# One SBUF input per VectorE instruction in a top-k search, and three query tiles moved between the tiles of a convolution

## The chip, the core and the metric

The kernel runs on one core of one Trainium2 chip, all in float32. The metric is the device time of one execution in microseconds, a median of several runs. The profile is of one execution; its times are counted from the span's first instruction. Engines are named as in the profile: PE is TensorE, PEld its weight loads, DVE is VectorE, ACT is ScalarE, POOL is GpSimd, SP is the engine that issues the transfers.

## The reference

One step of a two-layer encoder for a prompt of 1024 positions and a sample of 64 positions (with 512 cached ones), model width 1024. Layer 0 is what the change touches:

```
h = rmsnorm(x) * (1 + scale(c)) + shift(c)
q, k, v, ga, qi, ki, wi, gb, gc, xin, gz = split(h @ w_in)
score[q, s] = sum_h wi[q, h] * relu(qi[q, h] . ki[s])          # admissible keys only
keep the top 256 keys of each query (144 for the sample)
a = softmax(q . k / 8 over the kept keys) v * silu(ga)          # 8 heads of 64, 2 groups of keys
b = gb * conv3(gc * xin) * silu(gz)                             # causal, 3 taps
x += gate(c) * (concat(a, b) @ w_out)
```

Layer 1 is a gated unit with a spatial mix in chunks of 128 positions, and a final norm follows. Keys, values, index keys and the convolution's state are outputs too.

## The kernel before

The activations lie with features on partitions: 8 k tiles of 128 features by 1088 columns (1024 of the prompt, 64 of the sample). To be exact in float32, each operand is split into a high and a low part (`ah`, `al`, `w_hi`, `w_lo`), and a product is three matrix products. A column tile of a projection is 128 output features: 3 chunks of columns (364, 364, 360) by 8 k tiles by 3 products, so 72 matrix products. For each tile the weights come by a transfer from SP, ACT makes `w_hi` (L239), POOL makes `w_lo` (L240, two inputs), PE multiplies (L248, or L263 where the products are handed out a step at a time), and ACT moves each chunk from PSUM to SBUF (L784, L793).

Layer 0 goes through these stages. `scores` fills `S`, 128 partitions by 4800 columns: seven row blocks of 128 queries with 384, 512, 640, 768, 896, 1024 and 576 keys. `topk` then finds the k-th largest score of each row bit by bit: 8 rounds for the exponent, 23 for the mantissa, 31 in all. In a round the scores smaller than a candidate are counted row block by row block, then a few instructions on 1 to 4 columns decide the bit: `m` (L571), the step `g` (L578 for the exponent, L588 for the mantissa) and the candidate (L579, L590). There are three groups of row blocks (`GROUPS`) that go on independently. The four blocks of 512, 640, 768 and 576 keys are counted by VectorE in all rounds. Those of 896 and 1024 keys are counted by ACT in all rounds (a sum of signs, L565 and L568). That of 384 keys is counted by VectorE in the first 15 rounds and by ACT in the last 16. In the first 15 rounds the counts read `bias`, a bfloat16 copy of the scores' upper halves with k's sign (L529, one tensor input). In the last 16 they read `S` itself and multiply by k's sign on the way:

```
V.scalar_tensor_tensor(o, self.S[:, span(j)], col(sgn, j), thr.to_broadcast([P, SW[j]]),
                       op0=OP.mult, op1=OP.is_lt, accum_out=col(cv, j))
```

This is L531. Its second tensor input is the threshold, one column broadcast over the block, also in SBUF. All small tensors of the search (`cv`, `m`, `limd`, `lima`, `g`, `cand`, `step`) lie in SBUF.

Beside the search run 14 projection tiles: Q0, K, V, and for each quarter c of the convolution's features GZ (c > 0), GC and XIN. `gc` and `z`, where GC and XIN go, have one buffer each; K and V use them first. `conv` (L758 to L772) runs on POOL alone and ends with `bo *= y`. While it reads `gc` and `z`, the next GC tile can't be moved out of PSUM; there are five PSUM banks for these tiles, so PE can run five chunks ahead. When the thresholds `T` are there, `mask` (L614 to L619) turns each row block of `S` into 0 for chosen keys and a large negative number for the others, in `bias`, on VectorE alone.

Then comes attention, four head pairs with nine row blocks each: logits on PE (L632), bias and maximum on VectorE (L634), exponential on ACT (L637), the normalisation on POOL (L639), transposes and weighted values on PE (L662, L670). The queries of a pair are first stacked by `pair_stack` (ACT L710, POOL L711). Between the products of attention PE does the steps of the tiles in `ATTN_TILES`, one at a time, by fixed numbers (`RATE`). What is left is done behind attention. The first `BEFORE` = 255 steps are done ahead of attention: the tiles Q1, Q2 and Q3 with 72 each, and 39 of GB0.

The instructions are traced in program order, `topk` ahead of the tiles that run beside it. A planner with its own costs then sets the order on each engine, by readiness and then by program order. On the chip each engine keeps to that order.

Of the kernel before, what the change touches and what calls it, by code (L numbers as in the profile page):

```python
# [32 lines left out]
# chunks of columns: of the projections, and of those back to the residual, where a short one comes last  # L33
# [6 lines left out]
def pieces(w):  # L40
    """First columns of the pieces of 128 that cover w columns."""
    return [*range(0, w - P, P), w - P]


# column tiles of the even layer's projection, in the order in which they are computed
# [3 lines left out]
ATTN_TILES = [(Q_, 1), (Q_, 2), (Q_, 3), (GB, 0), (GB, 1), (GA, 0), (GB, 2), (GA, 1), (GB, 3), (GA, 2), (GA, 3)]  # L49


def even_tiles():
    col = {QI: 1280, KIWI: 1792, GA: 768, K_: 512, V_: 640, Q_: 0, GC: 2376, XIN: 2888, GB: 1864, GZ: 3400}
    order = [(QI, 0), (QI, 1), (QI, 2), (QI, 3), (KIWI, 0), (Q_, 0)] + [(GZ, c) for c in range(NGZ)]
    order += [(K_, 0), (V_, 0)]
    for c in range(4):
        order += [(GZ, c)] * (c >= NGZ) + [(GC, c), (XIN, c)]
# [10 lines left out]
# widths of the score rows: prompt blocks 2..7, then the sample  # L68
# [5 lines left out]
# k tiles of late modulation units done after the last two tiles of index queries  # L74
ADA_EARLY = (0, 27)
# gate tiles that fill the waits of the index scores
NGZ = 1
# products that keep the tensor engine's clock up while it waits for 1/rms and for the first modulation
WARM = (7, 3)
# the rows of each search that goes on by itself, and whether ScalarE counts in the first stage and in the second  # L80
# [3 lines left out]
UPPER_ACT = (4, 5)  # L84
SPANS = [slice(min(COL[j] for j in g[0]), max(COL[j] for j in g[0]) + 1) for g in GROUPS]
ORDER = [(0, 1, 2, 3, 4, 5, 6, 7)] + [(7, 0, 6, 1, 5, 2, 4, 3)] * 3
# matrix products of projections that fill the tensor engine's waits: before attention, and for each head pair
# after the logits of a chunk, after a group of weighted values and before it
BEFORE = 255
# [3 lines left out]
def cut(n):  # L93
    """Equal pieces of at most one bank."""
    k = (n + 511) // 512
    return k, n // k


class Trunk:
# [5 lines left out]
    # ------------------------------------------------------------------ helpers  # L105
# [12 lines left out]
    # ------------------------------------------------------------------ constants  # L118
# [21 lines left out]
    # units of 512 modulation columns: u < 4 hold shift and scale of two k tiles each, 4 and 5 the gate  # L140
# [5 lines left out]
    def ada_steps(self, l, u, raw, halt=False):  # L146
        """A unit, a k tile at a step; with halt another step before the transposition."""
# [26 lines left out]
    def ada_late(self, pool):  # L174
        """The units that the index phase leaves room for, a k tile at a step; their loads run ahead."""
# [25 lines left out]
    def pace(self, after, n):  # L201
        """n steps of the side work, behind one of the matrix products."""
# [40 lines left out]
    def product(self, ps, w, c0, c1, kts=range(KT)):  # L243
        """ps [P, c1-c0] = W^T act, in three products of the exact parts."""
# [6 lines left out]
    def steps(self, w, evac, chunks=range(NCH), n=2, tag="pj"):  # L251
        """A projection, n matrix products at a step."""
# [980 lines left out]
```

## Time and profile before

| | us |
|---|---|
| median of 3 runs | 1203.1 (1202.98 to 1203.14) |
| span of the profiled execution | 1200.9 |
| around the span (1203.1 less 1200.9) | 2.2 |
| VectorE busy in the span | 729.0 |
| PE busy in the span | 1098.8 |
| mean granted clock, share of full speed | 0.963 |

The profiled execution has no time of its own beside its span; the median stands for it. A line such as "348.58 2.79 DVE L531 ..." says when an instruction began, how long it took, on which engine and line, what it wrote and read, and in which shape; "x16 | 20.7, 1295 | 0.1" at a row's end is the count, the busy time in us, the mean of one in ns, and the idle time ahead of them.

### The profile page before, as it was taken

Reading aid. Unit: us, or ns where it says so; the run is one execution under the profiler, and the core shown is the slowest. Engines: PE = TensorE matmul, PEld = TensorE weight load, DVE = VectorE, ACT = ScalarE, POOL = GpSimd, SP = SyncE. Lnnn points to the kernel's source line nnn. Section 1 sums busy time; section 2 is a strip of 40 time slices with the busy share of each in tenths; the row PEclk is TensorE's granted clock in tenths of the full one; section 3 lists DMA queues with packets and bytes.
Section 4 is the critical chain, followed back from the end, with each engine's and each line's share of the span. In section 5 each row is a group of like instructions: output and inputs, shape, how many; then the busy total and the mean of one; then the engine's idle time right before and its main releaser. Section 6 shows DMA issues by size and latency. Waiting matters only on the chain.

```text
span 1200.9 us, 18882 instructions
## 1 busy us (share of the span) xinstructions
PE 1098.8 (91%) x7255; PEld 1054.6 (88%) x7255; DVE 729.0 (61%) x1663; ACT 513.6 (43%) x964; POOL 460.2 (38%) x454
## 2 busy tenths in 40 slices
PE   5899999695959885999999899999999999999997
PEld 4799689595958885988999899999999999999996
DVE  5602899999999798776775534431159036346133
ACT  5332784645665525677775533431221211235110
POOL 3632322344647673544542324641133210245121
PEclk9999999898979896999999899999999999999998
DMA  9646401110101010000000350211111210121012
GB/s 362 279 167 220 168 2 53 73 36 19 36 18 36 19 58 14 19 19 19 19 19 19 114 175 1 71 36 36 36 59 40 84 37 19 52 77 65 1 62 88
DMA packets 26074, 81.84 MB, mean 68 GB/s; under 512 B 3072, under 2 KB 9984, under 8 KB 23552
## 3 DMA queue, kind: packets, MB, share of 16 engines
q1 hardware_dynamic: 25984, 80.63, 19.2%
q8 instruction: 57, 0.93, 0.3%
q14 instruction: 33, 0.27, 0.1%
HBM read 74.50 MB, written 6.12 MB: 67 GB/s over the span
## 4 chain that ended last, share of the span: by engine, by line
PE 61%; DVE 25%; ACT 5%; issue 3%; POOL 2%; DMA 2%; SPq 0%; POOLq 0%; DVEq 0%; ACTq 0%
PE pj L248 26%; PE op L248 15%; DVE cum L531 6%; PE pj L263 6%; DVE cum L529 5%; PE av L670 3%; PE logit_ps L632 3%; PE p_ps L662 2%; DVE m L571 2%; PE ada_ps L154 1%; DVE g L588 1%; PE sgu_ps L1048 1%; DVE cum L616 1%; PE first L319 1%; POOL w_lo L240 1%
## 5 line engine op out<-in xcount | busy, mean ns | idle before, releaser
L248 PE MATMUL pj<-ah,w_hi 128*128 128x364 f32 (+1 forms) x984 | 331.0, 336 | 34.4 <-ACT gc L784 33.0
L248 PE MATMUL pj<-al,w_hi 128*128 128x364 f32 (+1 forms) x984 | 328.3, 334 | 0.0
L248 PE MATMUL pj<-ah,w_lo 128*128 128x364 f32 (+1 forms) x984 | 327.5, 333 | 0.0
L240 POOL TENSOR_TENSOR w_lo<-w_raw,w_hi 128x1024 fp32r<-128x1024 f32 x63 | 160.9, 2556 | 380.8 <-ACT w_hi L239 356.8
L248 PEld LDWEIGHTS pj<-ah,w_hi 128*128 128x128 f32 x984 | 188.8, 192 | 36.6 <-ACT gc L784 33.9
L248 PEld LDWEIGHTS pj<-al,w_hi 128*128 128x128 f32 x984 | 188.8, 192 | 0.0
L248 PEld LDWEIGHTS pj<-ah,w_lo 128*128 128x128 f32 x984 | 188.5, 192 | 0.3 <-issue 0.2
L248 PE MATMUL op<-ah,w_lo 128*128 128x448 f32 (+2 forms) x384 | 126.7, 331 | 3.2 <-POOL w_lo L240 3.2
L248 PE MATMUL op<-al,w_hi 128*128 128x448 f32 (+2 forms) x384 | 127.0, 331 | 0.4 <-DVE al L278 0.3
L248 PE MATMUL op<-ah,w_hi 128*128 128x448 f32 (+2 forms) x384 | 127.3, 331 | 0.0
L239 ACT ACTIVATE w_hi<-w_raw 128x1024 fp32r<-128x1024 f32 x69 | 72.7, 1056 | 108.6 <-PE pj L248 79.1
L988 DVE SCALAR_TENSOR_TENSOR x<-op,mod,x 128x192 f32<-128x192 f32 (+2 forms) x64 | 30.5, 497 | 109.0 <-PE op L248 109.0
L263 PE MATMUL pj<-ah,w_hi 128*128 128x364 f32 (+1 forms) x288 | 96.2, 334 | 0.0
L263 PE MATMUL pj<-al,w_hi 128*128 128x364 f32 (+1 forms) x288 | 95.2, 331 | 0.0
L263 PE MATMUL pj<-ah,w_lo 128*128 128x364 f32 (+1 forms) x288 | 95.2, 331 | 0.0
L639 POOL TENSOR_SCALAR S<-S,sm 128x384 f32<-128x384 f32 (+8 forms) x68 | 50.8, 753 | 85.1 <-DVE sm L638 73.7
L248 PEld LDWEIGHTS op<-ah,w_lo 128*128 128x128 f32 x384 | 73.4, 191 | 5.5 <-POOL w_lo L240 3.5
L531 DVE SCALAR_TENSOR_TENSOR cum<-S,sgn,cand 128x512 bf16<-128x512 f32 (+3 forms) x67 | 76.7, 1145 | 1.5
L248 PEld LDWEIGHTS op<-al,w_hi 128*128 128x128 f32 x384 | 73.3, 191 | 3.2 <-DVE al L278 1.1
L248 PEld LDWEIGHTS op<-ah,w_hi 128*128 128x128 f32 x384 | 73.4, 191 | 2.0
L996 POOL TENSOR_TENSOR acc<-acc,sq 128x448 f32<-128x448 f32 (+2 forms) x40 | 40.0, 999 | 91.4 <-ACT sq L994 90.7
L278 DVE TENSOR_TENSOR ptl<-p_ps,pth 128x512 fp32r<-128x512 f32 (+1 forms) x88 | 54.4, 621 | 20.0 <-ACT pth L277 18.7
(251 smaller groups left out, 2120.1 us busy)
## 6 DMA issues: line engine op xcount, KB each, us to landing
w_raw<-in_w SPq DMA_DIRECT2D x53, 512.0 KB, 3.5
ada<-in_ada_w SPq DMA_DIRECT2D x19, 1024.0 KB, 9.1
w_raw<-in_wo SPq DMA_DIRECT2D x16, 512.0 KB, 3.4
x<-in_x SPq DMA_DIRECT2D x8, 544.0 KB, 6.6
bo<-in_ada_w SPq DMA_DIRECT2D x4, 1024.0 KB, 6.8
x<-in_x SPq DMA_DIRECT2D x1, 1792.0 KB, 8.8
out_y<-x SPq DMA_DIRECT2D x1, 1792.0 KB, 6.6
x<-in_x SPq DMA_DIRECT2D x1, 1536.0 KB, 9.2
```

The costliest lines, as they stand in the source:

```text
L239: nc.scalar.activation(hi, raw, AF.Copy)
L240: (nc.gpsimd if lo_eng == "pool" else nc.vector).tensor_sub(lo, raw, hi)
L248: last = self.nc.tensor.matmul(ps, wt[:, kt, :], at[:, kt, c0:c1], start=n == 0, stop=n == len(mms) - 1)
L263: self.nc.tensor.matmul(ps, wt[:, kt, :], at[:, kt, a:b], start=kt == 0 and i == 0, stop=kt == KT - 1 and i == 2)
L278: (lo_eng or self.nc.vector).tensor_sub(lo, src, hi)
L529: V.tensor_scalar(o, self.bias[:, span(j)], thr, 0.0, op0=OP.is_lt, op1=OP.add, accum_out=col(cv, j))
L531: V.scalar_tensor_tensor(o, self.S[:, span(j)], col(sgn, j), thr.to_broadcast([P, SW[j]]), op0=OP.mult, op1=OP.is_lt, accum_out=col(cv, j))
L632: mm = nc.tensor.matmul(pt[:, 0:w], lhs, keys[i][:, g, s], start=i == 0, stop=i == 1)
L639: nc.gpsimd.tensor_scalar(p, p, st[:, 3:4], 0.0, op0=OP.mult, op1=OP.add)
L670: mm = nc.tensor.matmul(av[:, 0:m], self.vs[0:r, vbase + j, g, :], t[0:r, o:o + m], start=j == 0 and i == 0, stop=j == nj - 1 and i == 1)
L988: nc.vector.scalar_tensor_tensor(x[:, t, a:b], ps[:, a:b], self.mod[l][:, 16 + t, j:j + 1], x[:, t, a:b], op0=OP.mult, op1=OP.add)
L996: nc.gpsimd.tensor_add(acc, acc, sq)
```

## The change

Part one, in `topk`. The scores in `S` are multiplied in place by k's sign, once, by ACT; the bfloat16 copy is gone, and all counts of VectorE have the one form that reads `S` and takes the threshold as a scalar pointer. ACT's counts read `S` with a fixed scale. `limd`, `lima`, `g` and `step` move into a bank of PSUM (the one that weighted values use later), so that L571, L588, L590 and their like have one input in SBUF and one in PSUM; `g` is written to PSUM too. `mask` gets one more instruction per row block, on ACT, that gives the scores their own sign back.

Part two. Q1 stands behind V, Q2 behind the first XIN and Q3 behind the second; `BEFORE` is 0, so GB0's 39 steps go to attention's fill. Comments that the diff also removes are left out here.

```diff
-ATTN_TILES = [(Q_, 1), (Q_, 2), (Q_, 3), (GB, 0), (GB, 1), (GA, 0), (GB, 2), (GA, 1), (GB, 3), (GA, 2), (GA, 3)]
+ATTN_TILES = [(GB, 0), (GB, 1), (GA, 0), (GB, 2), (GA, 1), (GB, 3), (GA, 2), (GA, 3)]
-    order += [(K_, 0), (V_, 0)]
+    order += [(K_, 0), (V_, 0), (Q_, 1)]
-        order += [(GZ, c)] * (c >= NGZ) + [(GC, c), (XIN, c)]
+        order += [(GZ, c)] * (c >= NGZ) + [(GC, c), (XIN, c)] + [(Q_, c + 2)] * (c < 2)
-BEFORE = 255
+BEFORE = 0
...
+        small = self.bank("av", "small")
+        limd, lima, g = (small[:, i * NSB:(i + 1) * NSB] for i in range(3))
+        step = small[:, 32:32 + steps * NSB].rearrange("p (s j) -> p s j", j=NSB)
...
-        def smaller(j, thr, first):
-            o = junks[0][:, 0:SW[j]]
-            if first:
-                V.tensor_scalar(o, self.bias[:, span(j)], thr, 0.0, op0=OP.is_lt, op1=OP.add, accum_out=col(cv, j))
-            else:
-                V.scalar_tensor_tensor(o, self.S[:, span(j)], col(sgn, j), thr.to_broadcast([P, SW[j]]),
-                                       op0=OP.mult, op1=OP.is_lt, accum_out=col(cv, j))
+        def smaller(j, thr):
+            V.tensor_scalar(junks[0][:, 0:SW[j]], self.S[:, span(j)], thr, 0.0, op0=OP.is_lt, op1=OP.add,
+                            accum_out=col(cv, j))
...
-        top = self.S.bitcast(BF).rearrange("p (n e) -> p n e", e=2)[:, :, 1]
-        for j in range(NSB):
-            if j in UPPER_ACT:
-                nc.scalar.activation(self.bias[:, span(j)], top[:, span(j)], AF.Copy, scale=col(sgn, j))
-            else:
-                V.tensor_scalar(self.bias[:, span(j)], top[:, span(j)], col(sgn, j), None, op0=OP.mult)
-        V.tensor_scalar(nsg, m, -2.0, 1.0, op0=OP.mult, op1=OP.add)
+        for j in sum((g[0] for g in GROUPS), ()):
+            nc.scalar.activation(self.S[:, span(j)], self.S[:, span(j)], AF.Copy, scale=col(sgn, j))
         for lim, i in ((limd, 0), (lima, 2)):
-            V.tensor_sub(lim, lims[:, i + 1, :], lims[:, i, :])
-            V.tensor_mul(lim, lim, m)
-            V.tensor_add(lim, lim, lims[:, i, :])
+            V.tensor_sub(limx, lims[:, i + 1, :], lims[:, i, :])
+            V.tensor_mul(limx, limx, m)
+            V.tensor_add(lim, limx, lims[:, i, :])
...
     def mask(self, pool, j):
...
+        self.nc.scalar.activation(sl, sl, AF.Copy, scale=self.sgn[:, p])
...
                 do(V_, 0, into(vt))
+                do(Q_, 1, into(self.q[:, 1, :]))
...
                     self.conv(se, c, gc, z)
+                    if c < 2:
+                        do(Q_, c + 2, into(self.q[:, c + 2, :]))
```

## Rows read from the trace of the kernel before

**Rows 1.** The page, head.
```profile
span 1200.9 us, 18882 instructions
```

**Rows 2.** Busy time by stretch: us, each engine (instructions), granted clock, DMA share, GB/s.
```profile
182.00:402.00 220.00, 173.36 (x971) 171.24 (x971) 208.05 (x607) 126.59 (x228) 102.20 (x96) 0.88 0.11 37
402.00:461.00 59.00, 44.20 (x267) 43.75 (x265) 58.01 (x65) 11.40 (x22) 38.15 (x30) 0.90 0.12 39
461.00:470.00 9.00, 7.61 (x26) 6.50 (x26) 6.46 (x33) 8.01 (x25) 4.76 (x9) 0.50 0.05 15
470.00:640.00 170.00, 165.12 (x1131) 155.97 (x1130) 126.31 (x403) 122.43 (x257) 81.23 (x82) 1.00 0.06 18
```

**Rows 3.** Timeline of VectorE, the marks of search, mask and attention.
```profile
188.52 0.66 DVE L538 TENSOR_SCALAR sgn<-m 128x7 f32<-128x7 f32 x1
...
390.53 1.25 DVE L590 TENSOR_TENSOR T<-cand,g 128x4 f32<-128x4 f32 x1
...
402.58 0.16 DVE L590 TENSOR_TENSOR T<-cand,g 128x1 f32<-128x1 f32 x1
...
412.43 0.67 DVE L614 TENSOR_SCALAR_CACHE_REDUCE bias<-S,T,kneg 128x384 bf16<-128x384 f32 x1
...
461.47 0.28 DVE L634 CUSTOM_DVE_ANT_0 S<-logit_ps,corner 128x128 f32<-128x128 f32 x1
```

**Rows 4.** Timeline from 347 to 356 us, GpSimd's and VectorE's.
```profile
347.76 3.00 POOL L240 TENSOR_TENSOR w_lo<-w_raw,w_hi 128x1024 fp32r<-128x1024 f32 x1 [6.89 <-ACT w_hi L239]
348.58 2.79 DVE L531 SCALAR_TENSOR_TENSOR cum<-S,sgn,cand 128x576 bf16<-128x576 f32 x1
...
354.80 0.82 DVE L531 SCALAR_TENSOR_TENSOR cum<-S,sgn,cand 128x576 bf16<-128x576 f32 x1
```

**Rows 5.** Groups by line, VectorE, 180 to 412 us.
```profile
L531 DVE SCALAR_TENSOR_TENSOR cum<-S,sgn,cand 128x512 bf16<-128x512 f32 (+3 forms) x67 | 76.7, 1145 | 1.5
L529 DVE TENSOR_SCALAR_CACHE_REDUCE cum<-bias,cand 128x512 bf16<-128x512 bf16 (+4 forms) x75 | 60.6, 808 | 0.9
L588 DVE SCALAR_TENSOR_TENSOR g<-m,step 128x4 f32<-128x4 f32 (+2 forms) x69 | 20.4, 314 | 0.2
L571 DVE TENSOR_TENSOR m<-cv,lima 128x2 f32<-128x2 f32 (+1 forms) x47 | 16.2, 348 | 7.8 <-ACT junk L568 7.8
L571 DVE TENSOR_TENSOR m<-cv,limd 128x4 f32<-128x4 f32 (+1 forms) x46 | 13.6, 296 | 0.4
...
L578 DVE TENSOR_SCALAR g<-m 128x4 f32<-128x4 f32 (+2 forms) x24 | 8.5, 363 | 0.0
...
L545 DVE TENSOR_SCALAR bias<-S,sgn 128x384 bf16<-128x384 bf16 (+4 forms) x5 | 2.2, 503 | 0.0
```

**Rows 6.** One line, L588: durations in ns, min/median/max, first and last start.
```profile
L588 DVE SCALAR_TENSOR_TENSOR g<-m,step x69: 145/156/2317, 252.0 to 402.4; 128x4 f32<-128x4 f32 x23, 128x1 f32<-128x1 f32 x23, 128x2 f32<-128x2 f32 x23
```

**Rows 7.** One line, L166 (its first input lies in PSUM), as above.
```profile
L166 DVE TENSOR_TENSOR mod<-ada_ps,adab x20: 144/153/167, 23.8 to 149.6; 128x4 f32<-128x4 f32 x16, 128x8 f32<-128x8 f32 x4
```

**Rows 8.** Groups by line, VectorE, the stretch of the mask.
```profile
L616 DVE TENSOR_TENSOR_SCAN cum<-ones,cv,bias 128x384 bf16<-128x384 f32 (+6 forms) x7 | 14.7, 2096 | 0.0
...
L614 DVE TENSOR_SCALAR_CACHE_REDUCE bias<-S,T,kneg 128x384 bf16<-128x384 f32 (+6 forms) x7 | 6.4, 984 | 0.0
```

**Rows 9.** Waits of PE, 182 to 464 us: total, times, longest.
```profile
PE pj L248 <- ACT gc L784: 33.0, 3, 13.0
```

**Rows 10.** Timeline of GpSimd: the last conv's first and last instruction, then the query stack.
```profile
405.88 2.85 POOL L760 TENSOR_TENSOR z<-z,gc 128x1024 f32<-128x1024 f32 x1
...
428.58 0.58 POOL L772 TENSOR_TENSOR bo<-bo,gc 128x64 f32<-128x64 f32 x1
...
442.10 8.36 POOL L711 TENSOR_TENSOR qst<-q,qst 64x512 fp32r<-64x512 f32 x4
```

**Rows 11.** Timeline of ScalarE: the first chunk of Q1 and of Q2.
```profile
406.55 0.48 ACT L784 ACTIVATE q<-pj 128x364 f32<-128x364 f32 x1 [2.68 <-PE pj L263]
...
418.51 0.48 ACT L784 ACTIVATE q<-pj 128x364 f32<-128x364 f32 x1 [2.74 <-PE pj L263]
```

More of the change, by code (lines that the diff above doesn't have):

```diff
@@ L83 @@
 COL = {j: n for n, j in enumerate(sum((g[0] for g in GROUPS), ()))}
-UPPER_ACT = (4, 5)
 SPANS = [slice(min(COL[j] for j in g[0]), max(COL[j] for j in g[0]) + 1) for g in GROUPS]
 ORDER = [(0, 1, 2, 3, 4, 5, 6, 7)] + [(7, 0, 6, 1, 5, 2, 4, 3)] * 3
-BEFORE = 255
+BEFORE = 0
 RATE = ((1, 1, 3),) * 4
@@ L513, in topk @@
         nc.gpsimd.memset(tiny, 2.0 ** -126)
-        cv, m, sgn, nsg, limd, lima, T, cand, g, flag = (
-            t(n) for n in ("cv", "m", "sgn", "nsg", "limd", "lima", "T", "cand", "g", "flag"))
-        self.T, self.cv = T, cv
+        cv, m, sgn, limx, T, cand, flag = (t(n) for n in ("cv", "m", "sgn", "limx", "T", "cand", "flag"))
+        self.T, self.cv, self.sgn = T, cv, sgn
         junks = [self.cum, pool.tile([P, SEQ], BF, name="junk")]
+        small = self.bank("av", "small")
+        limd, lima, g = (small[:, i * NSB:(i + 1) * NSB] for i in range(3))
+        step = small[:, 32:32 + steps * NSB].rearrange("p (s j) -> p s j", j=NSB)
         def span(j):
@@ L523, in col @@
             return v[:, COL[j]:COL[j] + 1]
-        def smaller(j, thr, first):
-            o = junks[0][:, 0:SW[j]]
-            if first:
-                V.tensor_scalar(o, self.bias[:, span(j)], thr, 0.0, op0=OP.is_lt, op1=OP.add, accum_out=col(cv, j))
-            else:
-                V.scalar_tensor_tensor(o, self.S[:, span(j)], col(sgn, j), thr.to_broadcast([P, SW[j]]),
-                                       op0=OP.mult, op1=OP.is_lt, accum_out=col(cv, j))
+        def smaller(j, thr):
+            V.tensor_scalar(junks[0][:, 0:SW[j]], self.S[:, span(j)], thr, 0.0, op0=OP.is_lt, op1=OP.add,
+                            accum_out=col(cv, j))
         for j in range(NSB):
-            V.tensor_scalar(junks[0][:, 0:SW[j]], self.S[:, span(j)], 0.0, 0.0, op0=OP.is_lt, op1=OP.add,
-                            accum_out=col(cv, j))
+            smaller(j, 0.0)
         V.tensor_tensor(m, cv, lims[:, 1, :], op=OP.is_le)
         V.tensor_scalar(sgn, m, 2.0, -1.0, op0=OP.mult, op1=OP.add)
-        top = self.S.bitcast(BF).rearrange("p (n e) -> p n e", e=2)[:, :, 1]
-        for j in range(NSB):
-            if j in UPPER_ACT:
-                nc.scalar.activation(self.bias[:, span(j)], top[:, span(j)], AF.Copy, scale=col(sgn, j))
-            else:
-                V.tensor_scalar(self.bias[:, span(j)], top[:, span(j)], col(sgn, j), None, op0=OP.mult)
-        V.tensor_scalar(nsg, m, -2.0, 1.0, op0=OP.mult, op1=OP.add)
-        for lim, i in ((limd, 0), (lima, 2)):
-            V.tensor_sub(lim, lims[:, i + 1, :], lims[:, i, :])
-            V.tensor_mul(lim, lim, m)
-            V.tensor_add(lim, lim, lims[:, i, :])
-        for j in range(NSB):
-            smaller(j, col(tiny, j), True)
+        for j in sum((g[0] for g in GROUPS), ()):
+            nc.scalar.activation(self.S[:, span(j)], self.S[:, span(j)], AF.Copy, scale=col(sgn, j))
+        for lim, i in ((limd, 0), (lima, 2)):
+            V.tensor_sub(limx, lims[:, i + 1, :], lims[:, i, :])
+            V.tensor_mul(limx, limx, m)
+            V.tensor_add(lim, limx, lims[:, i, :])
+        for j in sum((g[0] for g in GROUPS), ()):
+            smaller(j, col(tiny, j))
         V.tensor_tensor(flag, cv, limd, op=OP.is_le)
@@ L555, in topk @@
         V.tensor_scalar(cand, tiny, exps[0], None, op0=OP.mult)
-        step = pool.tile([P, steps, NSB], F32, name="step")
         def count(n, first):
@@ L562, in count @@
                 if not act:
-                    smaller(j, col(cand, j), first)
-                elif first:
-                    nc.scalar.activation(junks[1][:, 0:SW[j]], self.bias[:, span(j)], AF.Sign, scale=-1.0 - 2.0 ** -10,
-                                         bias=col(cand, j), accum_out=col(cv, j))
+                    smaller(j, col(cand, j))
                 else:
-                    nc.scalar.activation(junks[1][:, 0:SW[j]], self.S[:, span(j)], AF.Sign, scale=col(nsg, j),
+                    nc.scalar.activation(junks[1][:, 0:SW[j]], self.S[:, span(j)], AF.Sign, scale=-1.0,
                                          bias=col(cand, j), accum_out=col(cv, j))
@@ L594, in topk @@
             if j in ACT_ROWS:
-                smaller(j, col(cand, j), False)
+                smaller(j, col(cand, j))
             else:
```

## Prediction

> **What bounds the kernel now.** I read the page first: a span of 1200.9 us [rows 1], in which PE is the busiest engine by far. Then I cut the span at the stages and asked for each engine's busy time [rows 2]. During attention (470 to 640 us) PE is busy for 165.1 of 170 us at full clock: that stage is PE's own, and any product added to its fill lengthens it. Ahead of it the picture is another. From 182 to 402 us, while the search runs, PE is busy for 173.4 of 220 us and idle for 46.6, but VectorE is busy for 208.1. From 402 to 461 PE has another 14.8 us of idle time, and VectorE is busy for 58.0 of 59. So the reader is to see that the way to attention is VectorE's: search, then mask, then attention.
>
> The marks on VectorE's timeline give the lengths [rows 3]. k's sign is known at 188.5. The four row blocks that VectorE counts are done at 390.5; the blocks that ScalarE counts come in at 402.6, so there is a tail of 12 us. The mask begins at 412.4, and attention's first instruction on VectorE starts at 461.5. PE's Q1, Q2 and Q3 (about 36 us) fill the mask's time and cost nothing there.
>
> Why the search takes 224 us shows in one pair of instructions [rows 4]. The same count of 576 columns takes 0.82 us at one place and 2.79 at another, and the long one ends just after a GpSimd subtraction of two SBUF tensors that began 0.8 us earlier and took 3.00. In groups [rows 5, 6]: L531, L588 and L571 have two tensor inputs in SBUF, and their means lie far above what they take undisturbed. For L588 the median is 156 ns, the mean 314 and the longest 2317: most run freely, a few are held for the length of a GpSimd instruction. L529, with one tensor input, ran in the same search beside the same kind of GpSimd work, and its mean of 808 ns for a mean width of 576 columns fits its widths.
>
> **The change, part by part.**
>
> The stretch that goes. L529's 75 counts cover 15 x 2880 = 43,200 columns in 60.6 us. L531's 67 cover 16 x 2496 + 2304 = 42,240, so by L529's rate they would take 59.3; they took 76.7: 17.4 us of stretch. L588: 69 x 0.156 = 10.8 of 20.4, so 9.6. L571, both groups: 93 x 0.156 = 14.5 of 29.8, so 15.3. L578 has one input, but shows the same long cases: 24 x 0.156 = 3.7 of 8.5, so 4.8; after the change it writes to PSUM. Together 47.1 us [rows 5, 6]. I take all of it, because each of these lines gets the form that L529 has, or one operand in PSUM. Not less than nothing goes: the new forms have no input that the old ones lack.
>
> The PSUM operands. 93 instructions of L571, 138 of L588 and L590, and 48 of L578 and L579 get an operand in PSUM, 279 in all. The trace has one small instruction of this kind: L166 reads PSUM and SBUF and takes 153 ns [rows 7], as much as the 156 of L588 with both in SBUF. So I count nothing for a read. No row shows VectorE writing to PSUM; 93 instructions will (`g`). Below, a write costs nothing more. Above, I let it cost as much again as the instruction, 0.15 us, so 14 us. I take nothing, by the nearest row. [...]
>
> The signs. Five VectorE instructions that made the upper halves go (2.2 us, L545) [rows 5]. In their place ScalarE rewrites 4800 columns of `S`. By 0.48 us for 364 columns [rows 11] that is 6.3 us, but VectorE follows block by block and waits only for the first, 0.7 us. Net 1.5 us less. In the mask the same 6.3 us on ScalarE run ahead of VectorE, whose L614 alone takes 6.4 for these columns [rows 8]; what shows is the first block, 0.5 us. ScalarE has the room: 126.6 of 220 us before [rows 2], now two times 6.3, less what it did for the upper halves, and three more tiles to move and split, by the same rate about 8 more; some 145 in a search shortened to about 175. That is dense, so I keep the tail of 12 us.
>
> The search then ends at 412.4 - 47.1 - 1.5 = 363.8. The mask is unchanged and still has two inputs in SBUF; it keeps its 49.0 us and gets 0.5. It ends at 413. Its bound below: the scan takes 14.7 us where L614 takes 6.4 for the same columns [rows 8], so at most some 8 us of it is stretch that could be gone if GpSimd were still. The search's bound below: no tail, 352.
>
> The moved tiles. Each takes 11.96 us on PE (from 406.55 to 418.51) [rows 11], 35.9 for three. They go where PE is idle: it waits three times for GC's chunks to leave PSUM, 33.0 us in total, 13.0 at the longest [rows 9], and Q2 and Q3 come just ahead of two of these; Q1 fills the wait behind V. If the holes took them all, XIN of the last quarter would end where it does now, near 402. ScalarE moves these chunks between its counts, and its counts wait for VectorE, so shorter holes come with a faster search: I take 398. Bounds: 402 + 35.9 - 46.6 = 391, and 410 if a hole stays. Their weights' transfers (three of 512 KB) go ahead by the same amount on SP; at a DMA share of 0.11 [rows 2] they cost nothing. On ScalarE and POOL each moves one split.
>
> What is late next. Behind the last XIN GpSimd has the last conv, 405.9 to 429.2, and the query stack, 8.4 us [rows 10]; before, both lay under Q1 to Q3 and the mask. From 398 the conv now ends near 425, and a stack behind it at 433. The stack's place is free once GC's last product has read its weights, 12 us earlier, so it may also go first. Even then the softmax's own GpSimd instruction (L639) shares the queue with the conv, and the first blocks run with gaps. So attention gets going between 413 (mask) and 433 (all of GpSimd first). I take 420, nearer the mask.
>
> The 39 steps of GB0 that were hidden ahead of attention now lie in a stage that is PE's own: 39 x 11.96 / 72 = 6.5 us added.
>
> The sum: attention starts at 420 in place of 461.5, so 41.5 less, and 6.5 more: 35 less. From the profiled execution's 1200.9 that is 1165.9. The runs' median lies 2.2 above its span, so 1168.
>
> **The rivals.**
>
> All at the mask's pace. ScalarE keeps up without the tail, the scans run freer, the stack comes first: 352 + 0.5 + 41 = 393, and PE is ready at 391. Attention at 395, 66.5 - 6.5 = 60 less, 1143. For it: the holes on ScalarE were waits for VectorE (7.8 us the other way only, at L571 [rows 5]). Against it: the last conv must go somewhere.
>
> GpSimd and small costs. The stack comes behind the conv, or VectorE pays for PSUM: 14 us bring the search to 378 and the mask's end to 427. Attention at 433, 28.5 - 6.5 = 22 less, 1181. [...]
>
> No gain: the stretch isn't tied to the second SBUF input, and VectorE instructions are held beside GpSimd whatever they read. Then the mask ends where it did, and the 39 steps are paid: 1203.1 + 6.5 = 1209.6, slower. It decides from the point where the mask ends after 455, so where less than 6.5 of the 47.1 us comes off. For it: L578, with one input, has its long cases too. Against it: L529 has none, and the long cases stand beside GpSimd's two-input work [rows 4, 5].
>
> **How the numbers follow.** The forecast, attention between 410 and 428 (1158 to 1176), gets 0.55; the fast rival 0.20; the slow one 0.19; no gain 0.06. Two runs differ by some 0.2% without cause, so 2.4 us is what can be told from no change. Only the last case holds the times at or above that, and a little of it lies in between: faster 0.93, same 0.02, slower 0.05. The range takes most of both neighbours, 1146 to 1186.
>
> **What would show it.** L531's place in the search should show a mean of some 0.85 to 0.95 us a count and L571 and L588 near 156 ns, with no case above 1 us; rows of 200 ns and more would mean PSUM's price. The first L614 should stand near 364, the first L634 near 420, the last XIN's end near 398. PE's waits for GC should be down to one. Behind the mask, VectorE or PE waiting for GpSimd is the slow rival's sign; a tail over 12 us between VectorE's last count and ScalarE's is a ScalarE that has become the bound. The prediction is wrong if the long cases stay.

## The result, and the profile after

The changed kernel takes 1174.8 us (median of 4 runs, 1173.57 to 1176.73), the kernel before 1203.0 beside it: ratio 0.9769, 95% interval 0.9756 to 0.9783. The forecast was 1168, with a range of 1146 to 1186. So it is faster, as forecast, by 28.3 us where 35 were forecast.

The page's head, then the busy time by stretch (columns as in [rows 2]):

```profile
span 1172.8 us, 18888 instructions
...
182.00:380.00 198.00, 197.02 (x1186) 196.64 (x1186) 167.86 (x617) 138.43 (x251) 96.26 (x99) 1.00 0.15 49
...
380.00:428.00 48.00, 3.16 (x12) 2.18 (x10) 47.60 (x52) 5.46 (x11) 34.34 (x27) 0.55 0.04 14
...
428.00:460.00 32.00, 29.35 (x174) 26.74 (x175) 24.24 (x88) 24.46 (x57) 19.08 (x23) 0.88 0.04 13
...
460.00:620.00 160.00, 156.15 (x1073) 147.72 (x1072) 112.47 (x358) 111.32 (x235) 67.35 (x68) 1.00 0.06 18
```

From 182 to 380 us PE is busy for 197 of 198 us, at full clock, where it was idle for 46.6 of 220 at a mean of 0.88 [rows 2]. The three waits for GC [rows 9] are gone. Then comes a hole that was not there before: from 380 to 428 PE is busy for 3.2 of 48 us, while VectorE is busy throughout and GpSimd for 34.3.

The marks on VectorE's timeline, to be laid beside [rows 3]; a bracket holds the idle time ahead and what ended it:

```profile
188.34 0.67 DVE L534 TENSOR_SCALAR sgn<-m 128x7 f32<-128x7 f32 x1
...
368.53 0.16 DVE L577 TENSOR_TENSOR T<-cand,small 128x4 f32<-128x4 f32 x1
...
374.24 0.16 DVE L558 TENSOR_TENSOR m<-cv,small 128x2 f32<-128x2 f32 x1 [5.55 <-ACT junk L555]
...
375.37 0.15 DVE L577 TENSOR_TENSOR T<-cand,small 128x1 f32<-128x1 f32 x1
...
380.14 0.67 DVE L602 TENSOR_SCALAR_CACHE_REDUCE bias<-S,T,kneg 128x384 bf16<-128x384 f32 x1
...
427.70 0.28 DVE L622 CUSTOM_DVE_ANT_0 S<-logit_ps,corner 128x128 f32<-128x128 f32 x1
```

The mask begins at 380.1 (412.4 before), attention's first instruction at 427.7 (461.5). That is 33.8 us earlier, and the span is 28.1 shorter. VectorE's groups in the search, beside [rows 5]:

```profile
L528 DVE TENSOR_SCALAR_CACHE_REDUCE cum<-S,cand 128x512 bf16<-128x512 f32 (+5 forms) x142 | 119.0, 838 | 2.3
...
L558 DVE TENSOR_TENSOR m<-cv,small 128x4 f32<-128x4 f32 (+2 forms) x93 | 14.2, 152 | 22.6 <-ACT junk L555 22.4
...
L575 DVE SCALAR_TENSOR_TENSOR small<-m,small 128x4 f32<-128x4 f32 (+2 forms) x69 | 11.2, 163 | 1.3
...
L565 DVE TENSOR_SCALAR small<-m 128x4 f32<-128x4 f32 (+2 forms) x24 | 3.8, 160 | 0.2
```

None of these groups is stretched any more. But `m` (L558) is preceded by 22.4 us of idle time that ends with a count of ScalarE (7.8 before). At the other end of the gap to attention stands GpSimd; its last conv's first and last instruction and the stack, beside [rows 10]:

```profile
383.85 2.00 POOL L748 TENSOR_TENSOR z<-z,gc 128x1024 f32<-128x1024 f32 x1
...
408.40 0.32 POOL L760 TENSOR_TENSOR bo<-bo,gc 128x64 f32<-128x64 f32 x1
...
408.80 8.34 POOL L699 TENSOR_TENSOR qst<-q,qst 64x512 fp32r<-64x512 f32 x4
```

### The profile page after: what moved, and what is told of

It is laid out like the page before. It is cut to its first block, busy times and chain, and to the rows that moved or that the text cites. A ratio compares the mean times of both kernels' runs of the same rounds, so it can differ in the third digit from the quotient of the medians.

```text
span 1172.8 us, 18888 instructions
## 1 busy us (share of the span) xinstructions
PE 1086.2 (93%) x7255; PEld 1042.1 (89%) x7255; DVE 677.2 (58%) x1657; ACT 518.5 (44%) x976; POOL 449.4 (38%) x454
## 4 chain that ended last, share of the span: by engine, by line
PE 83%; DVE 8%; ACT 4%; POOL 2%; issue 2%; DMA 1%; SPq 0%; POOLq 0%; DVEq 0%; ACTq 0%
PE pj L247 44%; PE op L247 15%; PE pj L262 7%; PE av L658 3%; PE logit_ps L620 3%; PE p_ps L650 3%; PE ada_ps L153 2%; PE score_ps L427 1%; PE sgu_ps L1040 1%; DVE cum L604 1%; PE first L318 1%; PE score_ps L428 1%; POOL hf L329 1%; DVE al L277 1%; DMA w_raw<-in_w 1%
## 5 line engine op out<-in xcount | busy, mean ns | idle before, releaser
L247 PE MATMUL pj<-ah,w_hi 128*128 128x364 f32 (+1 forms) x1056 | 349.5, 331 | 1.0 <-ACT w_hi L238 1.0
L247 PE MATMUL pj<-al,w_hi 128*128 128x364 f32 (+1 forms) x1056 | 347.4, 329 | 0.0
L247 PE MATMUL pj<-ah,w_lo 128*128 128x364 f32 (+1 forms) x1056 | 346.8, 329 | 0.0
L247 PEld LDWEIGHTS pj<-ah,w_hi 128*128 128x128 f32 x1056 | 198.5, 188 | 1.9 <-ACT w_hi L238 1.3
L247 PEld LDWEIGHTS pj<-ah,w_lo 128*128 128x128 f32 x1056 | 198.4, 188 | 0.3 <-issue 0.2
L247 PEld LDWEIGHTS pj<-al,w_hi 128*128 128x128 f32 x1056 | 198.6, 188 | 0.0
L528 DVE TENSOR_SCALAR_CACHE_REDUCE cum<-S,cand 128x512 bf16<-128x512 f32 (+5 forms) x142 | 119.0, 838 | 2.3
L620 PE MATMUL logit_ps<-kp,qst 128*128 128x384 f32 (+5 forms) x192 | 50.0, 370 | 48.0 <-POOL qst L699 31.0
L555 ACT ACTIVATE junk<-S,cand 128x896 bf16<-128x896 f32 (+2 forms) x78 | 77.6, 995 | 19.8 <-DVE m L558 16.0
L620 PEld LDWEIGHTS logit_ps<-kp,qst 128*128 128x128 f32 x192 | 33.5, 201 | 52.1 <-POOL qst L699 32.6
L262 PE MATMUL pj<-ah,w_hi 128*128 128x364 f32 (+1 forms) x216 | 72.3, 335 | 0.0
```

Source lines behind the costliest of these rows:

```text
L247: last = self.nc.tensor.matmul(ps, wt[:, kt, :], at[:, kt, c0:c1], start=n == 0, stop=n == len(mms) - 1)
L262: self.nc.tensor.matmul(ps, wt[:, kt, :], at[:, kt, a:b], start=kt == 0 and i == 0, stop=kt == KT - 1 and i == 2)
L528: V.tensor_scalar(junks[0][:, 0:SW[j]], self.S[:, span(j)], thr, 0.0, op0=OP.is_lt, op1=OP.add, accum_out=col(cv, j))
L555: nc.scalar.activation(junks[1][:, 0:SW[j]], self.S[:, span(j)], AF.Sign, scale=-1.0, bias=col(cand, j), accum_out=col(cv, j))
L620: mm = nc.tensor.matmul(pt[:, 0:w], lhs, keys[i][:, g, s], start=i == 0, stop=i == 1)
```

## Experiments

The first column of this table says which half of the search's edit and which tile order a kernel has; the marks are the first instruction of the mask and of attention on VectorE, the last logits' instruction there, and the first product of the output projection.

| counts / small tensors / tile order | run | median, us | mask | attention | last logits | output |
|---|---|---|---|---|---|---|
| two inputs / SBUF / before | before | 1203.1 | 412.4 | 461.5 | 639.4 | 673.6 |
| two inputs / SBUF / moved | tiles_only | 1210.7 | 407.0 | 464.3 | | |
| one input / SBUF / moved | small_sbuf | 1192.8 | 394.5 | 446.0 | | |
| two inputs (late rounds) / PSUM / moved | count_two | 1191.4 | 394.8 | 442.1 | | |
| one input / PSUM / moved | after | 1174.8 | 380.1 | 427.7 | 607.1 | 647.1 |
| one input / PSUM / before | search_only | 1162.2 | 381.9 | 420.5 | 600.7 | 634.9 |
| as after, 39 steps of GB ahead | fill39 | 1170.7 | 380.8 | 428.8 | 608.0 | 642.2 |
| as search_only, 60 steps of GB ahead | fill60 | 1164.0 | 380.0 | 418.9 | 602.9 | 636.0 |
| as search_only, 216 steps of GB ahead | search_fill | 1155.8 | 379.5 | 425.6 | 601.5 | 620.2 |

**The search without the tiles.** The changed search and mask; tiles and `BEFORE` as before the change:

```diff
-ATTN_TILES = [(GB, 0), ...
+ATTN_TILES = [(Q_, 1), (Q_, 2), (Q_, 3), (GB, 0), ...
...
-BEFORE = 0
+BEFORE = 255
...
-                do(Q_, 1, into(self.q[:, 1, :]))
...
```

> The changed search and mask with the tile order of before: Q1 to Q3 and 39 steps of GB0 again ahead of attention. Theory A (the gain is the stretch that left VectorE, attention waits for the mask's end): without the three tiles PE reaches its last XIN before 380, Q1 to Q3 and the 39 steps (42 us) end before 425 under the tail of the search and the mask, so attention starts near 428 as in the changed kernel, and its fill is 6.5 us shorter: 1166 to 1172. Rival B (the gain is the three tiles in PE's holes): Q1 to Q3 are late again, attention starts after 440, 1185 to 1200.

1162.2 us (1160.5 to 1163.6), ratio to before 0.966 (0.9639 to 0.9682): 12.6 us faster than the whole change, and 41.0 faster than before. Theory A holds in kind, and its range was too high: attention starts at 420.5, where it had 428. Busy time by stretch:

```profile
182.00:362.00 180.00, 179.02 (x1079) 178.61 (x1078) 157.37 (x573) 125.02 (x230) 102.51 (x114) 1.00 0.15 48
...
382.00:413.00 31.00, 8.89 (x56) 8.69 (x54) 30.79 (x42) 3.93 (x6) 8.22 (x5) 0.71 0.07 21
```

PE is busy for 179 of 180 us in the search although no tile was moved there: the faster search alone closed the holes. And the mask, with GpSimd busy for 8.2 of 31 us, takes 38.6 us where the changed kernel's takes 47.6. Its groups, the changed kernel first:

```profile
L604 DVE TENSOR_TENSOR_SCAN cum<-ones,cv,bias 128x384 bf16<-128x384 f32 (+6 forms) x7 | 15.0, 2140 | 0.0
...
L606 DVE SCALAR_TENSOR_TENSOR bias<-S,T,bias 128x384 bf16<-128x384 f32 (+6 forms) x7 | 8.6, 1229 | 0.2
...
L605 DVE SCALAR_TENSOR_TENSOR bias<-cum,bias 128x384 bf16<-128x384 bf16 (+6 forms) x7 | 8.5, 1207 | 0.0
...
L607 DVE TENSOR_SCALAR bias<-bias 128x384 bf16<-128x384 bf16 (+6 forms) x7 | 4.0, 566 | 0.0
```

The same groups without the moved tiles:

```profile
L604 DVE TENSOR_TENSOR_SCAN cum<-ones,cv,bias 128x384 bf16<-128x384 f32 (+6 forms) x7 | 11.5, 1637 | 0.0
...
L606 DVE SCALAR_TENSOR_TENSOR bias<-S,T,bias 128x384 bf16<-128x384 f32 (+6 forms) x7 | 6.5, 932 | 0.2
...
L605 DVE SCALAR_TENSOR_TENSOR bias<-cum,bias 128x384 bf16<-128x384 bf16 (+6 forms) x7 | 6.1, 866 | 0.0
...
L607 DVE TENSOR_SCALAR bias<-bias 128x384 bf16<-128x384 bf16 (+6 forms) x7 | 2.2, 315 | 0.0
```

These four give 3.5 + 2.1 + 2.4 + 1.8 = 9.8 us. In the changed kernel they ran beside the last conv (383.9 to 408.7) and the stack; without the moved tiles the last conv ended at 370, under the search, and only one `w_lo` and the stack are left beside the mask.

**The tiles without the search.** The edit of `even_tiles`, `ATTN_TILES`, `BEFORE` and `layer0` alone.

> The search and mask of before with the moved tiles and no step of a projection ahead of attention. Theory A: VectorE's search and mask keep their length, attention still starts near 461, and the 39 steps of GB0 are added to attention's fill: 1203 to 1211, so slower or the same. Rival B: the tiles carry a good part of the gain, attention starts before 445: 1180 to 1195.

1210.7 us (1210.3 to 1211.3), ratio 1.0063 (1.0039 to 1.0087): slower by 0.6%, within theory A's range, but not quite by its way. The mask begins 5.5 us earlier and takes 50.0 us until its last instruction ends at 457.0 (48.7 before). Attention could start then, but GpSimd's last conv has slid behind the moved tiles and ends at 462.2, and the query stack comes behind it. PE's wait for the stack, the stack, and attention's first instruction on VectorE:

```profile
PE logit_ps L632 <- POOL qst L711: 33.9, 2, 33.6
...
462.30 5.57 POOL L711 TENSOR_TENSOR qst<-q,qst 64x512 fp32r<-64x512 f32 x4
...
464.34 0.29 DVE L634 CUSTOM_DVE_ANT_0 S<-logit_ps,corner 128x128 f32<-128x128 f32 x1 [7.34 <-PE logit_ps L632]
```

So VectorE is idle for 7.3 us, and this kernel's attention waits for GpSimd, as in the prediction's slow rival.

**Half of the search's edit at a time.** First `limd`, `lima`, `g` and `step` back in SBUF:

```diff
-        small = self.bank("av", "small")
-        limd, lima, g = (small[:, i * NSB:(i + 1) * NSB] for i in range(3))
+        limd, lima, g = (t(n) for n in ("limd", "lima", "g"))
+        step = pool.tile([P, steps, NSB], F32, name="step")
```

> The changed kernel, with limd, lima, g and step back in SBUF, so that the decisions m, g and the candidate have two SBUF inputs again; the counts stay in their new form. Theory A (an instruction with two SBUF inputs is held for the length of a GpSimd instruction that runs beside it): their means go back from near 155 to near 300 ns, some 25 us of VectorE's time in the search, of which the idle time that VectorE has there for ScalarE's counts (some 30 us) hides a part; the first instruction of the mask moves from 380 to between 390 and 405, time 1183 to 1200. Rival B (the place of small tensors does not matter, the counts' form did all): within 3 us of the changed kernel, 1172 to 1178, means below 180 ns.

1192.8 us (1192.6 to 1194.1): theory A. VectorE's groups in that search:

```profile
L527 DVE TENSOR_SCALAR_CACHE_REDUCE cum<-S,cand 128x512 bf16<-128x512 f32 (+5 forms) x142 | 118.9, 837 | 2.4
...
L576 DVE TENSOR_TENSOR cand<-cand,g 128x2 f32<-128x2 f32 (+2 forms) x66 | 26.0, 415 | 0.4
...
L557 DVE TENSOR_TENSOR m<-cv,lima 128x2 f32<-128x2 f32 (+1 forms) x47 | 18.6, 407 | 4.1 <-ACT junk L554 3.9
...
L574 DVE SCALAR_TENSOR_TENSOR g<-m,step 128x1 f32<-128x1 f32 (+2 forms) x69 | 17.7, 276 | 0.1
...
DVE m L557 <- ACT junk L554: 3.9, 5, 2.6
```

The counts keep their 837 ns; the three small groups shown go from 152 to 163 ns up to 276 to 415. VectorE's waits for ScalarE fall to the last row's figure, from 22.4: part of the stretch is hidden there, and the mask begins 14.3 us later. Then the counts of the last 16 rounds in their old form (times a column of ones):

```diff
...
+        def smaller(j, thr, two=False):
+            if two:
+                V.scalar_tensor_tensor(junks[0][:, 0:SW[j]], self.S[:, span(j)], col(one, j),
+                                       thr.to_broadcast([P, SW[j]]), op0=OP.mult, op1=OP.is_lt,
+                                       accum_out=col(cv, j))
...
-                    smaller(j, col(cand, j))
+                    smaller(j, col(cand, j), not first)
```

> The changed kernel, with VectorE's counts of the last 16 rounds in the two-input form of before (score times a column of ones, compared with the threshold broadcast from SBUF); the small tensors stay in PSUM. Theory A: these 64 counts go from a mean of 0.84 to about 1.1 us, 17 us more for VectorE, partly hidden by its waits for ScalarE; the small instructions stay near 155 ns; first mask instruction 385 to 397, time 1179 to 1192. Rival B (only the small instructions' place counted): within 3 us of 1174.8.

1191.4 us (1189.4 to 1191.6): theory A, though the stretch is larger than I had put it:

```profile
L531 DVE SCALAR_TENSOR_TENSOR cum<-S,one,cand 128x512 bf16<-128x512 f32 (+1 forms) x64 | 82.1, 1283 | 1.2
...
L565 DVE TENSOR_TENSOR m<-cv,small 128x4 f32<-128x4 f32 (+2 forms) x93 | 14.0, 151 | 10.3 <-ACT junk L562 10.3
...
L582 DVE SCALAR_TENSOR_TENSOR small<-m,small 128x4 f32<-128x4 f32 (+2 forms) x69 | 11.2, 162 | 1.2
```

The small ones stay near 150 to 160 ns; the 64 counts mean 1283. With the moved tiles in all four, the two halves are worth 17.9 and 19.3 us alone and 35.9 together (1210.7, 1192.8, 1191.4, 1174.8): they nearly add up. The mask's first instruction, which the stack of the first of these four can't delay, comes 12.5, 12.1 and 26.8 us earlier.

**Less work on GpSimd.** The kernel before, `conv` cut to its small copies and one product:

```diff
-        G.tensor_mul(z[:, 2:2 + SEQ], z[:, 2:2 + SEQ], gc[:, 0:SEQ])
...
-            G.tensor_mul(self.bo[:, c, s], self.bo[:, c, s], y)
+        G.tensor_mul(self.bo[:, c, SO:TC], self.bo[:, c, SO:TC], gc[:, SO:TC])
```

> The kernel before, with the convolution's arithmetic on GpSimd left out (only its two small copies per quarter and one product of 64 columns stay, so the second half of layer 0's output is not the reference's); GpSimd still makes w_lo for each tile. Theory A (VectorE's two-input instructions are held while GpSimd works on SBUF): conv is 60 of some 100 us of GpSimd's work in the search, so about half of the stretch goes: the counts L531 from 1145 to about 1000 ns, L588 from 314 to about 235, first mask instruction between 385 and 400 in place of 412, time 1172 to 1190. Rival B (the two-input form is slow by itself, whatever runs beside it): the means stay within 5%, first mask instruction above 408, time above 1193.

1169.8 us (1169.4 to 1170.2), the mask's first instruction at 384.1:

```profile
L531 DVE SCALAR_TENSOR_TENSOR cum<-S,sgn,cand 128x512 bf16<-128x512 f32 (+3 forms) x67 | 66.8, 996 | 1.7
...
L588 DVE SCALAR_TENSOR_TENSOR g<-m,step 128x4 f32<-128x4 f32 (+2 forms) x69 | 13.7, 219 | 0.2
```

Not one VectorE instruction of the search was edited, and the means fell from 1145 and 314 ns [rows 5]. So it is what runs on GpSimd that holds them (theory A; time and mask even come a little below its ranges).

The trace of the kernel before says the same instruction by instruction. Of the 279 small instructions L571, L578, L579, L588 and L590, 54 begin inside a GpSimd instruction with 0.15 us or more of it to go. 27 of these take over 0.3 us, and each of the 27 ends within 0.03 us of the end of a GpSimd instruction. Two pairs, GpSimd's first:

```profile
215.98 2.39 POOL L240 TENSOR_TENSOR w_lo<-w_raw,w_hi 128x1024 fp32r<-128x1024 f32 x1 [23.76 <-DVE m L571]
216.73 1.66 DVE L578 TENSOR_SCALAR g<-m 128x2 f32<-128x2 f32 x1
...
243.81 2.39 POOL L240 TENSOR_TENSOR w_lo<-w_raw,w_hi 128x1024 fp32r<-128x1024 f32 x1 [14.68 <-ACT w_hi L239]
244.47 1.75 DVE L571 TENSOR_TENSOR m<-cv,limd 128x4 f32<-128x4 f32 x1
```

Six of the 27 end with a GpSimd multiplication that has one tensor input (L768, L770), so not only GpSimd's two-input work holds. In the changed kernel 114 of the 279 begin so, and none takes over 0.17 us. Undisturbed, the old count is no slower than the new one: the medians for 512, 640 and 768 columns are 752, 885 and 1019 ns for L531 before, and 747, 879 and 1008 for L528 after. So rival B is out.

**ScalarE as the new bound.** The row block of 384 keys counted by VectorE in all rounds:

```diff
-GROUPS = (((1, 2, 3, 6), 0, 0), ((4, 5), 1, 1), ((0,), 0, 1))
+GROUPS = (((1, 2, 3, 6), 0, 0), ((4, 5), 1, 1), ((0,), 0, 0))
```

> The changed kernel, with the row block of 384 keys counted by VectorE in the last 16 rounds too, so that ScalarE counts two blocks in every round. A round takes 4.6 us when nothing waits and 5.5 on the mean. Theory A (ScalarE is the bound of the changed search, its queue holds counts behind work that waits for PE): 0.8 us less on ScalarE per round and shorter waits outweigh 0.7 more on VectorE; search the same or up to 8 us shorter, time 1166 to 1175. Rival B (VectorE's own work still sets the round): 16 counts of 0.69 us more, 11 us, time 1180 to 1187.

1177.2 us (1175.3 to 1179.4), between the two. The mask begins at 380.9 (380.1 in the changed kernel), and VectorE still waits 20.3 us for ScalarE's counts (22.4): 16 counts more on VectorE and 16 fewer on ScalarE change nothing, so neither engine's sum of counts sets the round. What may is seen on ScalarE's timeline in the changed kernel, ahead of the wait that ends at 374.24:

```profile
367.52 0.81 ACT L772 ACTIVATE gc<-pj 128x364 f32<-128x364 f32 x2
...
368.61 0.47 ACT L772 ACTIVATE gc<-pj 128x360 f32<-128x360 f32 x1 [0.28 <-PE pj L247]
...
368.97 1.59 ACT L601 ACTIVATE S<-S,sgn 128x768 f32<-128x768 f32 x2
...
370.46 1.03 ACT L555 ACTIVATE junk<-S,cand 128x896 bf16<-128x896 f32 x1
...
372.60 0.48 ACT L781 ACTIVATE z<-pj 128x364 f32<-128x364 f32 x1 [1.01 <-PE pj L247]
...
372.97 1.14 ACT L555 ACTIVATE junk<-S,cand 128x1024 bf16<-128x1024 f32 x1
```

Between two counts stand chunks that wait for PE, and the mask's own sign instructions (L601). The candidate of the counts of 896 and 1024 keys is there at 367.8 (VectorE's L577); they begin at 370.46 and 372.97, behind what stands ahead of them in the queue. In the whole changed search ScalarE waits 31.5 us for PE, at chunks and high parts; in the search before, where PE had holes, it was 2.6. To take something out of that queue, the base of the first run, with the weights' high parts of these tiles on GpSimd:

```diff
+        if self.hi_pool:
+            nc.gpsimd.tensor_copy(hi, raw)
+        else:
             nc.scalar.activation(hi, raw, AF.Copy)
```

> The same base, with the high parts of the weights of the tiles beside the search made by GpSimd instead of ScalarE. Theory (the changed search is held by ScalarE's queue: a high part that waits there for PE to free its place holds the counts behind it, and VectorE waits 20 us for counts): VectorE's waits for ScalarE's counts fall from 20 to below 12 us, first mask instruction from 382 to between 368 and 376, time 1150 to 1157. Rival (the loop from candidate to count to decision, or VectorE's own work, sets the rounds): first mask instruction 380 or later, time 1160 to 1168.

1170.2 us (1169.6 to 1172.0): 8 slower than its base. The theory is right for the search and wrong for the time. VectorE's wait in the base, then in this run, the mask's first instruction, one of its groups, and the stretch of the mask (columns as in [rows 2]):

```profile
DVE m L558 <- ACT junk L555: 20.1, 18, 5.2
...
DVE m L562 <- ACT junk L559: 7.3, 15, 2.7
...
363.16 0.68 DVE L606 TENSOR_SCALAR_CACHE_REDUCE bias<-S,T,kneg 128x384 bf16<-128x384 f32 x1
...
L611 DVE TENSOR_SCALAR bias<-bias 128x384 bf16<-128x384 bf16 (+6 forms) x7 | 8.6, 1231 | 0.0
...
362.00:419.00 57.00, 38.66 (x218) 37.86 (x218) 56.42 (x56) 12.91 (x27) 47.11 (x30) 0.85 0.10 31
```

The search ends 18.7 us earlier (363.2 in place of 381.9), but with GpSimd busy for 47 of 57 us beside it the mask takes 55.9 us in place of 38.6, and attention begins at 419.1, only 1.4 earlier. Attention then takes 186.5 us in place of 180.3: PE was busy for 163 of 180 us beside the search (179 in the base) and has 70 products more left for it (1218 against 1148). So what stands in ScalarE's queue did hold the search. Which part of it held most is not shown: the run takes out the high parts' work and their waits together, and with PE behind, only 39 chunks are moved before the mask begins, where it was 53.

**Steps ahead of attention.** The changed kernel with 39 steps of GB0 there again (`BEFORE = 39`):

> The changed kernel with 39 steps of GB0 ahead of attention, as before the change. PE is idle there from 380 to 428. If the prediction's term is right (attention is PE's own stage, each step in it costs its length), the time falls by 6.5 us to 1168; rival: attention is not bound by PE, or the products' evacuations on VectorE lengthen the mask by as much, 1173 to 1176.

1170.7 us (1170.6 to 1170.7), 4.1 less, between the two. The table shows where: from attention's first instruction to the last logits it is 179.1 us, 179.4 without; from there to the output projection 34.2 in place of 40.0. The steps lie behind attention, not in it. With the base of the first run and many more, GB ahead of GA (`BEFORE = 432`):

> The search alone (as in the run with the tile order of before), but 432 steps ahead of attention: Q1 to Q3 and the first three tiles of GB, whose order is changed so that all GB come before GA. In that run PE was idle from 391 to 421 while VectorE made the mask. 177 steps more take 29.4 us and fit. Nine evacuations of 0.5 us are added to VectorE's mask time, so attention starts near 425. Theory (each step taken out of attention gives back its length, less what VectorE's own work of 132 in 180 us then sets): 20 to 25 us faster than the 1162 of that run, 1137 to 1145. Rival (attention's pace is set by its chain of VectorE, ScalarE and GpSimd, the fill sat in gaps): 1158 to 1166.

1155.8 us (1154.1 to 1156.2), ratio 0.9604 (0.9587 to 0.962). Neither: it is 6.4 faster than its base, where 20 to 25 were forecast. With evacuations and weights beside it, the mask is 7.6 us longer (46.1). Attention itself takes 175.8 us in place of 180.3 with 293 steps in it in place of 385, so its pace isn't set by the fill alone: 92 steps at 0.166 us would be 15. The output projection starts 14.7 earlier, and of that 7 are lost again behind it (the span is 7.6 shorter); why is not shown. Fewer steps, so ordered that none waits in attention (`BEFORE = 276`):

> The changed search with the tile order of before (as in the first experiment), but 60 steps of GB0 ahead of attention instead of 39, and GB2 ahead of GA0, so that no step in attention finds only a tile that must wait. In that run 99 steps lay behind attention, 27 more than the 72 of GA3 that can't come sooner. Theory (steps that stand behind attention cost their length, those within it almost none): 27 x 0.166 = 4.5 us less, 1156 to 1160. Rival (what comes behind attention waits for transfers and evacuations anyway): within 2 us of 1162.2.

1164.0 us (1163.2 to 1165.4): nothing gained, the rival. From the last logits to the output projection it is 33.1 us in place of 34.2, and attention takes 184.1 in place of 180.3.

**A shorter mask, and a mask within attention.** On the base of the first run, the comparisons for equality on GpSimd:

```diff
-        V.tensor_scalar(bi, sl, thr, self.kneg[:, p], op0=OP.is_gt, op1=OP.add, accum_out=c)
-        V.tensor_scalar(bi, sl, thr, None, op0=OP.is_equal)
+        V.tensor_scalar(cum, sl, thr, self.kneg[:, p], op0=OP.is_gt, op1=OP.add, accum_out=c)
+        self.nc.gpsimd.tensor_scalar(bi, sl, thr, 0.0, op0=OP.is_equal, op1=OP.add)
```

> The same base, with the seven comparisons for equality in the mask (6.9 us on VectorE) done by GpSimd, one SBUF input each, into the place that VectorE's first comparison no longer writes. Theory (attention starts when VectorE has finished the mask, nothing else): 5 to 7 us off the mask of 38.6 us, attention's first instruction on VectorE from 420.5 to about 414.5, time 1155 to 1158. Rival (GpSimd's comparisons hold VectorE, or the first scan waits for them): the mask keeps 36 us or more, 1160 to 1164.

1163.7 us (1162.5 to 1165.5): the rival. GpSimd's group, and the scans beside it:

```profile
L603 POOL TENSOR_SCALAR bias<-S,T 128x384 bf16<-128x384 f32 (+6 forms) x7 | 18.7, 2695 | 7.0 <-ACT S L601 7.0
...
L604 DVE TENSOR_TENSOR_SCAN cum<-ones,cv,bias 128x384 bf16<-128x384 f32 (+6 forms) x7 | 14.2, 2026 | 1.0 <-POOL bias L603 1.0
```

VectorE sheds 6.9 us, but its two-input work (L604, L605 and L606) takes 31.9 us, with these 18.7 us of GpSimd's beside it, where it took 24.1 in the base, and the mask takes 42.5 us. Last, each row block's mask just ahead of the block that needs it:

```diff
-                for j in range(NSB):
-                    self.mask(se, j)
...
                     for b in ORDER[t]:
+                        for j in MASKS[b] if t == 0 else ():
+                            self.mask(ap, j)
                         self.attend(ap, st, t, b)
```

> A version meant to beat both kernels: the changed search with the tile order of before (first experiment, 1162.2), and each row block's mask traced just ahead of the block of the first head pair that needs it, or that overwrites its scores, instead of all masks ahead of attention; the running counts of the mask lie in the place of a gate tile that is not needed yet. VectorE then still compares all rows first (14 us), but has only the first block's other four instructions and the second's scan (some 4 us) left before attention's first instruction: from 420.5 to about 400. The other 20 us of the mask stand between attention's instructions. Theory (VectorE has idle time in attention, 48 of 180 us, so a part of the mask hides there): the last logits of attention come 8 to 14 us earlier than in that run, time 1148 to 1155. Rival (the first head pair becomes VectorE's own and gives all of it back): 1160 to 1165.

1156.6 us (median of 5, 1154.3 to 1158.5), ratio 0.9615 (0.9596 to 0.9633). Attention's first instruction comes at 396.6, its last logits at 593.2, 7.5 us before its base's: just short of the 8 to 14, and the time lies between the theory's range and the rival's. It and the run with 432 steps can't be told apart; both beat the changed kernel by 18 to 19 us.

## Why the prediction was right, and where it was off

**The stretch.** Right, line by line: the counts went from 137.3 to 119.0 us (18.3, forecast 17.4), `m` from 29.8 to 14.2 (15.6; 15.3), the mantissa's `g` from 20.4 to 11.2 (9.2; 9.6), the exponent's from 8.5 to 3.8 (4.7; 4.8). Together 47.8, where 47.1 were forecast. The half-edits show the second SBUF input as the cause (three groups of small instructions at 276 to 415 ns in place of 152 to 163, the 64 late counts at 1283 in place of 862); the run without the convolution (L531 from 1145 to 996 ns) and the 27 long cases show GpSimd as the one that holds. "No gain" is out.

**PSUM.** Nothing, as L166's row said: 152, 155 and 163 ns with an operand in PSUM, the last one written there too. The 14 us that I had let stand above, for the writes, did not come: `g`, written to PSUM, took 163 and 160 ns (L575, L565), where the medians before were 156 and 162.

**The signs.** As small as forecast: VectorE stood 0.6 us ahead of its first counts of signed scores (forecast 0.7) and 0.1 ahead of the mask's first comparisons (0.5). But they also stand in ScalarE's queue: two of them, 1.59 us, lie ahead of the last count of 896 keys.

**The search's end.** Here the first term was mis-sized: forecast 363.8, measured 380.1. "That is dense, so I keep the tail of 12 us" was the wrong conclusion. VectorE's work shrank as forecast, but its waits for ScalarE's counts grew from 7.8 to 22.4 us, 14.6 of the 16.3 missed. The counts stand in one queue with chunks and high parts that wait for PE (31.5 us in this search, 2.6 before); with the high parts out of it (and the tile order of before) the search ends at 363.2. The sign that the prediction named, a tail over 12 us, did not show it: the tail shrank to 6.8 us (368.53 to 375.37), and most of the waits stood inside the rounds.

**The mask.** 47.6 us measured, 49.5 forecast. But I kept the old length as if it were the mask's own. The bound (8 us of stretch) was near, and too small: with GpSimd busy for 8 of 31 us it takes 38.6, which is 10.4 less than before.

**The moved tiles.** Two steps failed. The holes close by themselves when the search is faster; I wrote so ("shorter holes come with a faster search") and took 4 us for it. The last XIN ends at 380.5, ahead of my lower bound of 391, for which I had counted idle time and left out the clock: at a granted 0.88 of full speed PE took 0.1785 us of busy time per product before (173.36 / 971), at 1.00 it takes 0.1661 (197.02 / 1186), some 15 us over 1186 products. The other step is the last conv. I had it end at 425 beside the mask and cost nothing but its own place; it ends at 408.7, and its price is on VectorE: 9 us of mask (47.6 against 38.6).

**Attention's start.** 427.7, forecast 420. The stack came behind the conv, as in the slow rival, but was ready at 417.1; VectorE's mask was last. That 420 came so near is partly luck. The search ended 16.3 us late, the mask was 1.9 shorter, and the 7 us that I had put between the mask's end and attention for GpSimd were not needed.

**The 39 steps.** Forecast 6.5 us, in attention; measured 5.8 (40.0 against 34.2), behind it, of which 4.1 show in the time. So the size was near for another reason than the one given. The step "that stage is PE's own, and any product added to its fill lengthens it" failed twice. The steps per block are fixed by `RATE` (385 start between the two marks before, 390 after), so attention's length is nearly the same (178.0 us before, 179.4 after) and what is left over stands behind it. And where 92 steps fewer ran in it, it was only 4.4 us shorter.

**The sum.** 33.8 earlier, 5.8 given back: 28 in place of 35. The sum counted the moved tiles as free. Part one alone brought 41.0, and part two cost 12.6 of it: in the spans 10.9, of which 7.2 at attention's start, 5.8 behind attention, and 2.1 the other way in and after it.

## What to carry to other kernels

Where VectorE and GpSimd run side by side, count each VectorE instruction's SBUF inputs. Here the limits and steps that moved to PSUM brought the small instructions to 152 to 163 ns (276 to 415 from SBUF), and the threshold that became a scalar pointer brought the late counts to 862 (1283 with two inputs); with the moved tiles the two were worth 17.9 and 19.3 us alone and 35.9 together. When one engine gets faster, ask again which holes the old order was made for (PE was busy for 179 of 180 us beside the faster search with no tile moved), and what GpSimd work slides under the two-input instructions that are left (the last conv here, and 9 us of mask). An engine that was 70% busy (ScalarE: 138 of 198 us) still held up VectorE here (22.4 us of waits; 7.3 in place of 20.1 with the high parts out of the queue), through what its queue puts ahead of the instruction that is waited for.

## What the runs showed of the hardware that was not expected

One tensor input is not always enough. L607, a plain multiplication of a bfloat16 block, took 315 ns on the mean where GpSimd was mostly still (busy for 8 of 31 us), 566 in the changed kernel (GpSimd busy for 34 of 48 us) and 1231 (there L611) where it was busy for 47 of 57, while the counts, which also write a sum, kept 837 and 838 ns in the two searches shown (GpSimd busy for 96 of 198 us in the changed one). In the changed kernel's mask two forms with one tensor input stand beside GpSimd's work: L602, which writes a sum, took 867 ns for 576 columns and 1067 for 768, in step with its widths; L603, which writes none, took 601 for 768 and 1507 for 576. What decides it is not shown. L578's long cases before [rows 5] had one tensor input and no sum either: three of 24 took 1.44 to 2.33 us, and each ended within 0.03 us of a GpSimd instruction.

The hold goes both ways: the last conv took 24.9 us under the mask (383.85 to 408.72), and 17.0 under the changed search (350.82 to 370.26 in the run without the moved tiles, less 2.4 for one `w_lo` between). And a comparison on GpSimd was dear: 18.7 us for 4800 columns, 3.9 ns each, where its multiplication by a pointer takes 0.70 us for 512 (L758 in the base of that run), 1.4 ns each. How much of the 18.7 was waiting for VectorE's scans beside it stays open.
